# 320 dense tokens and 64 more gathered ones, with all gates built by matmuls, in an encoder step on one core

## The chip, the core and the metric

One core of a Trainium2 chip runs the whole step in one launch. The metric is device time in microseconds (us). The engines are PE (TensorE, with its weight loads PEld), DVE (VectorE), ACT (ScalarE), POOL (GpSimd) and SP (SyncE, which issues transfers). Each works through its own queue in order; semaphores connect them.

## The reference, cut to what matters

544 tokens of width 1024 go through one layer: 512 frames of a new stream (the prompt) and 32 frames of a running one (the sample). The part that the change touches is the second half of the layer:

```python
def peer_block(xb, w_query, keys_1, keys_2, u_tab, v_tab):      # 8 heads, 128 x 128 experts
    qy = (xb @ w_query).reshape(n, 8, 2, 128)
    s1, s2 = scores of the two halves of qy against keys_1, keys_2     # (n, 8, 128) each
    t1, i1 = top_k(s1, 16);  t2, i2 = top_k(s2, 16)
    top, sel = top_k(t1[:, None] + t2[None, :], 16)                    # of 256 pairs
    idx = i1 * 128 + i2 of the chosen pairs                            # 16 experts per head
    g = softmax(top)
    act = gelu(u_tab[idx] . xb)
    return sum over heads and experts of (g * act) * v_tab[idx]

h = layer_norm(alpha * x + token_mixer(x))      # attention and a linear recurrence, merged, projected
y = layer_norm(alpha * h + peer_block(h))
```

A token needs 8 × 16 = 128 of the 16384 experts. All arithmetic is in fp32.

## The kernel before

The tokens are S (32 sample frames) and P0 to P3 (128 prompt frames each). A first mixer runs S, P0 and P1 (288 columns), a second one P2 and P3 (256 columns). A matrix product in full precision is made of three: `split` cuts an operand into a high part (ACT, line 115) and a low part, which is the operand less the high part (line 119, DVE or, for the share `POOL_SHARE`, POOL), and `mm3` (lines 161, 164 and 165) multiplies high by high, low by high and high by low.

For the experts there are two ways. A **dense** token is multiplied with all experts: `up(b)` multiplies block b of table u (128 experts) with the normalized columns of the dense tokens, `hDh` and `hDl`, and takes the gelu; `down(b)` multiplies the result with the gates of this block (zero for experts that were not chosen), splits it, and multiplies with block b of table v. Before, P0, P1 and P2 are dense: 384 columns, 24 matmuls of 384 columns in `up`, 18 of 512 columns in `down`. For a **gathered** token POOL fetches the chosen rows of both tables by an indirect DMA (1 MB for 128 rows), DVE takes a dot product (line 1070), and DVE adds the weighted row to a sum (line 1082). S (packed four times, so 32 steps) and P3 (128 steps) are gathered.

`route(t, h)` finds the 16 experts of head h for the tokens t, mostly on DVE. The gates of the dense tokens have to be brought into the form experts × tokens. Before, there are two ways for that too. For P0 and P1 POOL writes each gate into a zeroed matrix in DRAM, by 256 indirect DMAs (`scatter`, line 998), behind 32 fills with zeros; `down` reads it back as `gt`. For P2 `gate_steps` makes one-hot matrices of four tokens at a time (DVE, tile `hot`, lines 1034 and 1038), multiplies them on TensorE (line 1042) and copies the result out. Routes and builds are put into `bg`, a list from which the matrix work takes a piece now and then at the rates `MIX_RATE` and `OUT_RATE`. The loop `experts` makes `up(it)` and, 29 iterations later (`AHEAD`), `down(it - 29)`:

```python
for it in range(EARLY, NK + AHEAD - LAST):
    if it < NK:
        up(it)
    b = it - AHEAD
    ...
    if b >= 0:
        p = down(b)
        for i in range(NDT):
            p(i)
```

So first only table u is read, then both, then only table v. The subtraction for the low part of both tables (line 1156) is on DVE. A gather is also paced on the load of the iteration's table block.

Of the kernel before, what the change touches and what calls it, by code (L numbers as in the profile page):

```python
# [23 lines left out]
F32 = mybir.dt.float32  # L24
# [9 lines left out]
P = 128  # L34
D = 1024
# [19 lines left out]
POOL_SHARE = (1, 5), (0, 1)  # L55
MIX_RATE = (6, 5), (3, 2)
MERGE_RATE = (1, 3)
OUT_RATE = (3, 2), (1, 1)
# [4 lines left out]
class Tok:  # L63


    def __init__(self, name, col, n, dense=None, prompt=None):
        self.name, self.col, self.n, self.dense, self.prompt = name, col, n, dense, prompt
        self.rep = P // n
        self.nh = H // self.rep
        self.ns = self.nh * TOPK  # L70
        self.done = 0

# [5 lines left out]
         toks=[Tok("S", 0, 32), Tok("P0", 32, 128, 0, 0), Tok("P1", 160, 128, 128, 128)]),  # L78
    dict(c0=288, n=256, p0=256, np=256, off=0,
         att=[Tok("P2", 0, 128, prompt=256), Tok("P3", 128, 128, prompt=384)],  # L80
         toks=[Tok("P2", 0, 128, 256, 256), Tok("P3", 128, 128, None, 384)]),
]
ND = 384
NDT = ND // P
ND0 = TS + ND
NS = 256
GT, GB = 16, 16
FILL, EARLY = 3, 4
AHEAD = 29
# [12 lines left out]
class Build:  # L102
    def __init__(self, tc, A):
        self.tc, self.nc, self.A = tc, tc.nc, A
        self.nsplit = 0
        self.pool_share = (1, 1)
        self.bg, self.tick, self.rate = [], -4, (1, 1)
        self.scatters, self.late, self.ready = {}, [], {}
        self.acts = {}

# [85 lines left out]
    def run(self):  # L196
        with ExitStack() as es:
# [6 lines left out]
            with tc.tile_pool(name="psm", bufs=3, space=PSUM) as self.psm, \  # L204
                    tc.tile_pool(name="kv", bufs=1) as self.kv, \
                    tc.tile_pool(name="wst", bufs=3) as self.wst:
                with tc.tile_pool(name="broA", bufs=1) as bro:
                    self.open(0, lambda s, name: self.keep.tile([P, KD, ND0], F32R, tag="hD" + s, name=name + s)[:, :, :288], bro)
                    self.load_first()
                    self.mixer(0)  # L210
                with tc.tile_pool(name="mTB", bufs=1) as mpool:
                    with tc.tile_pool(name="broB", bufs=1) as bro:
                        self.open(1, lambda s, name: mpool.tile([P, KD, 256], F32R, tag="mT" + s, name=name + s), bro)
# [6 lines left out]
    def open(self, i, tile_, bro):  # L220

        g = GROUPS[i]
        g["mT"] = lambda name: [tile_(s, name) for s in "hl"]
# [6 lines left out]
    def constants(self):  # L230
# [20 lines left out]
        self.iotaK = const.tile([P, 2, NK], F32, name="iotaK")  # L251
        for i, st in enumerate((NK, 1)):
            nc.gpsimd.iota(self.iotaK[:, i], pattern=[[st, NK]], base=0, channel_multiplier=0,
                           allow_small_or_imprecise_dtypes=True)

        self.tcol = const.tile([P, NDT], F32, name="tcol")
        nc.gpsimd.iota(self.tcol, pattern=[[P, NDT]], base=0, channel_multiplier=1,
                       allow_small_or_imprecise_dtypes=True)

        self.sel = const.tile([P, TS], F32, name="sel")  # L260
        nc.vector.tensor_reduce(out=self.sel, in_=self.ident.rearrange("p (g t) -> p t g", t=TS),
                                axis=AX.X, op=OP.add)

        self.G = self.dram.tile([NE * NS, 1], F32, name="gatemat")
        self.G2 = self.dram.tile([P // GT, P, NK * GT], F32, name="gatemat2")
        self.hS = self.dram.tile([ND, D], F32, name="hspill")
        zero = self.vtile(F32, [P, D], "zero")
        nc.gpsimd.memset(zero, 0.0)
        flat = self.G.rearrange("(p n) o -> p (n o)", p=P)
        self.zeroing = []  # L270

        def fill(c):
            self.zeroing.append(self.after_load(nc.sync.dma_start(flat[:, c * D:(c + 1) * D], zero)))
        self.bg += [lambda c=c: fill(c) for c in range(NE * NS // P // D)]
# [70 lines left out]
    def mixer(self, i):  # L345
# [390 lines left out]
    def rows_of_h(self, g, pool):  # L736
        nc, A = self.nc, self.A
        for t in g["toks"]:

            t.h = (self.keep if t.dense is None else pool).tile([P, D], F32, name="h" + t.name)  # L740
# [56 lines left out]
    def scale_rows(self, toks, eng):  # L797

        for t in toks:
            eng.tensor_tensor(out=t.h, in0=t.h, in1=self.g1, op=OP.mult)  # L800
            eng.tensor_tensor(out=t.h, in0=t.h, in1=self.b1, op=OP.add)
            if t.dense is not None:
                self.nc.sync.dma_start(self.hS[t.dense:t.dense + t.n], t.h)
# [541 lines left out]
```

## Time and profile before

| | |
|---|---|
| median of three runs | 1834.27 us (1832.07 to 1834.3) |
| profiled execution | 1832.22 us, span 1830.4 us |
| busy: PE, DVE, ACT, POOL | 1681.0, 1399.3, 866.9, 702.7 us |
| mean granted clock of TensorE | 0.963 |
| bytes moved | 442.97 MB |

The span begins with the first instruction of the profile. The first mixer with its projection and queries lies before about 330 us, the second with its projection from there to about 559, the queries of P2 and P3 to 637, then table u alone to 823, both tables to 1657, and table v with the final normalization to the end.

### The profile page before, as it was taken

Reading aid. Unit: us, or ns where it says so; the run is one execution under the profiler, and the core shown is the slowest. Engines: PE = TensorE matmul, PEld = TensorE weight load, DVE = VectorE, ACT = ScalarE, POOL = GpSimd, SP = SyncE. Lnnn points to the kernel's source line nnn. Section 1 sums busy time; section 2 is a strip of 40 time slices with the busy share of each in tenths; the row PEclk is TensorE's granted clock in tenths of the full one; section 3 lists DMA queues with packets and bytes.
Section 4 is the critical chain, followed back from the end, with each engine's and each line's share of the span. In section 5 each row is a group of like instructions: output and inputs, shape, how many; then the busy total and the mean of one; then the engine's idle time right before and its main releaser. Section 6 shows DMA issues by size and latency. Waiting matters only on the chain.

```text
span 1830.4 us, 26792 instructions
## 1 busy us (share of the span) xinstructions
PE 1681.0 (92%) x9448; PEld 1513.2 (83%) x9448; DVE 1399.3 (76%) x3187; ACT 866.9 (47%) x1723; POOL 702.7 (38%) x463
## 2 busy tenths in 40 slices
PE   8999999994989999919999999999999999998787
PEld 8889879984778999918898799999998989997565
DVE  6634779883976789719999878887888888886667
ACT  7644445782645674504555434443444444332333
POOL 2110236888888888862221112221222222121110
PEclk9999999997998999959999999999999999999999
DMA  9863736674475657649989689889999889897673
GB/s 318 281 233 100 226 99 161 157 164 63 57 185 121 147 117 179 164 105 349 333 297 326 238 321 334 342 339 348 320 333 361 330 313 335 332 345 286 249 263 108
DMA packets 159158, 442.97 MB, mean 242 GB/s; under 512 B 51064, under 2 KB 78376, under 8 KB 137520
## 3 DMA queue, kind: packets, MB, share of 16 engines
q1 hardware_dynamic: 93472, 265.76, 43.3%
q0 software_dynamic: 59904, 167.93, 29.5%
q10 hardware_dynamic: 5648, 7.58, 1.2%
q8 instruction: 74, 1.21, 0.3%
q14 instruction: 60, 0.49, 0.1%
HBM read 409.80 MB, written 31.36 MB: 241 GB/s over the span
## 4 chain that ended last, share of the span: by engine, by line
PE 65%; DVE 7%; DMA 4%; POOL 4%; ACT 4%; issue 2%; SPq 0%; DVEq 0%; ACTq 0%; POOLq 0%
PE y L161 9%; PE y L164 9%; PE u L161 9%; PE y L165 9%; PE u L164 9%; PE u L165 8%; POOL gatemat L998 4%; PE mm L161 3%; PE mm L164 3%; PE mm L165 3%; DMA gat<-peer_uv,idxP 2%; PE y L1042 1%; DVE wl L119 1%; PE x L895 1%; ACT vh L1155 1%
## 5 line engine op out<-in xcount | busy, mean ns | idle before, releaser
L998 POOL DMA_INDIRECT gatemat<-gateP,idxP x256 | 441.9, 1726 | 94.8 <-issue 73.3
L1059 POOL DMA_INDIRECT gat<-peer_uv,idxP x128 | 159.8, 1249 | 601.5 <-DMA ur<-u_chunk 191.4
L165 PE MATMUL u<-hDh,ul 128*128 128x384 f32 x992 | 335.8, 339 | 42.3 <-DVE ul L1156 42.2
L161 PE MATMUL u<-hDh,uh 128*128 128x384 f32 x992 | 339.7, 342 | 9.2 <-DVE hS L1099 4.5
L164 PE MATMUL u<-hDl,uh 128*128 128x384 f32 x992 | 336.3, 339 | 0.0
L161 PE MATMUL y<-vh,pwh 128*128 128x512 f32 x768 | 281.6, 400 | 25.5 <-ACT vh L1155 25.4
L164 PE MATMUL y<-vl,pwh 128*128 128x512 f32 x768 | 301.4, 396 | 0.7 <-DVE vl L1156 0.7
L165 PE MATMUL y<-vh,pwl 128*128 128x512 f32 x768 | 299.6, 396 | 0.0
L119 DVE TENSOR_TENSOR wl<-raw,wh 128x1024 fp32r<-128x1024 f32 (+1 forms) x134 | 164.4, 1229 | 86.9 <-ACT wh L115 86.3
L165 PEld LDWEIGHTS u<-hDh,ul 128*128 128x128 f32 x992 | 187.4, 189 | 43.8 <-DVE ul L1156 43.8
L1070 DVE SCALAR_TENSOR_TENSOR gat<-gat,hP 128x1024 f32<-128x1024 f32 x128 | 156.2, 1221 | 85.1 <-DMA gat<-peer_uv,idxP 85.0
L115 ACT CAST wh<-raw 128x1024 fp32r<-128x1024 f32 (+1 forms) x140 | 145.0, 1039 | 151.7 <-PE mm L164 87.9
L161 PEld LDWEIGHTS u<-hDh,uh 128*128 128x128 f32 x992 | 187.7, 189 | 15.6 <-DVE hS L1099 5.4
L161 PEld LDWEIGHTS y<-vh,pwh 128*128 128x128 f32 x768 | 144.8, 191 | 60.6 <-ACT vh L1155 32.6
L164 PEld LDWEIGHTS u<-hDl,uh 128*128 128x128 f32 x992 | 187.7, 189 | 4.2
L1155 ACT CAST uh<-ur 128x1024 fp32r<-128x1024 f32 x124 | 129.9, 1047 | 104.0 <-DMA ur<-u_chunk 98.4
L1156 DVE TENSOR_TENSOR vl<-vr,vh 128x1024 fp32r<-128x1024 f32 x128 | 155.9, 1220 | 24.0 <-ACT vh L1155 16.3
L165 PEld LDWEIGHTS y<-vh,pwl 128*128 128x128 f32 x768 | 145.3, 189 | 33.9
L1082 DVE SCALAR_TENSOR_TENSOR accP<-gat,actP,accP 128x1024 f32<-128x1024 f32 x127 | 162.4, 1279 | 13.0 <-ACT actP L1073 12.3
L164 PEld LDWEIGHTS y<-vl,pwh 128*128 128x128 f32 x768 | 145.7, 190 | 31.6 <-DVE vl L1156 1.1
L1156 DVE TENSOR_TENSOR ul<-ur,uh 128x1024 fp32r<-128x1024 f32 x124 | 151.1, 1219 | 25.1 <-ACT uh L1155 17.4
L161 PE MATMUL mm<-xTh,wh 128*128 128x288 f32 (+1 forms) x512 | 155.5, 304 | 12.0 <-ACT wh L115 6.8
(366 smaller groups left out, 3310.3 us busy)
## 6 DMA issues: line engine op xcount, KB each, us to landing
vr<-peer_v SPq DMA_DIRECT2D x128, 512.0 KB
ur<-u_chunk SPq DMA_DIRECT2D x124, 512.0 KB
raw<-w_chunk SPq DMA_DIRECT2D x63, 512.0 KB
gatemat<-zero SPq DMA_DIRECT2D x32, 512.0 KB
raw<-w_q SPq DMA_DIRECT2D x32, 512.0 KB
gt<-gatemat SPq DMA_DIRECT2D x128, 128.0 KB
raw<-w_up SPq DMA_DIRECT2D x16, 512.0 KB
raw<-w_out SPq DMA_DIRECT2D x16, 512.0 KB
```

The costliest lines, as they stand in the source:

```text
L115: nc.scalar.copy(h, src)
L119: eng.tensor_tensor(out=l, in0=src, in1=h.bitcast(F32), op=OP.subtract)
L161: first = nc.tensor.matmul(out, lh, rh, start=start, stop=False)
L164: nc.tensor.matmul(out, lh, rl, start=False, stop=False)
L165: return first, nc.tensor.matmul(out, ll, rh, start=False, stop=stop)
L895: nc.tensor.matmul(ps[:, i], qT[:, t.col:t.col + t.n], self.keysT[:, half], start=True, stop=True)
L998: i = nc.gpsimd.indirect_dma_start(out=self.G, out_offset=bass.IndirectOffsetOnAxis(ap=t.idx[:, j:j + 1], axis=0), in_=t.gate[:, j:j + 1], ...
L1059: i = nc.gpsimd.indirect_dma_start(out=r.rearrange("p i d -> p (i d)"), out_offset=None, in_=A["peer_uv"], in_offset=bass.IndirectOffsetOn ...
L1070: nc.vector.scalar_tensor_tensor(out=r[:, 0], in0=r[:, 0], scalar=1.0, in1=t.h, op0=OP.mult, op1=OP.mult, accum_out=a)
L1082: nc.vector.scalar_tensor_tensor(out=v["acc"], in0=r[:, 1], scalar=a, in1=v["acc"], op0=OP.mult, op1=OP.add)
L1155: nc.scalar.copy(h, raw)
L1156: nc.vector.tensor_tensor(out=l, in0=raw, in1=h.bitcast(F32), op=OP.subtract)
```

## The change

- P0 is cut: its first 64 tokens (P0a, packed twice, 64 steps) are gathered, and 320 tokens stay dense. P0's second half goes through `down` with a 128-wide operand that holds low and high side by side, so that two matmuls per half take the place of three, and a block takes 16 matmuls.
- All gates are made by `gate_steps`; scatters, zero fills and `gt` are gone. Of the two one-hot matrices both are made by one DVE operation each (128x512); the product with the gate is made by POOL.
- The steps of S and the first of P0a, the routes of S, P0 and P1 and the builds of P0 and P1 go into the background of the second mixer. The tiles for it lie in `ring`, in the space of `hD`: two slots for gathered rows and one buffer `hot` for the one-hots. The normalized columns of P0 and P1 are kept in DRAM meanwhile (`hN`) and read back before table u.
- In the second mixer POOL takes half of the subtractions of the weights, the memset of `qa` is on DVE, and in `experts` POOL makes the subtraction of table v (all but the last four blocks). `AHEAD` is 36.

```diff
-POOL_SHARE = (1, 5), (0, 1)
-MIX_RATE = (6, 5), (3, 2)
+POOL_SHARE = (1, 5), (1, 2)
+MIX_RATE = (6, 5), (3, 1)
+MIX_GATHER = 1, 3
 MERGE_RATE = (1, 3)
-OUT_RATE = (3, 2), (1, 1)
+OUT_RATE = (3, 2), (2, 1)
...
-ND = 384
+HALF = 64
+ND = 384 - HALF
...
-GT, GB = 16, 16
+GT, GB, UN = 16, 8, 64
-AHEAD = 29
+AHEAD = 36
...
-                (nc.vector if self.first else nc.gpsimd).memset(self.qa[DH:DH + 2], 1.0)
+                nc.vector.memset(self.qa[DH:DH + 2], 1.0)
...
+    def early_rows(self, toks):
+        S, P0, P1 = toks
+        ring = keep.tile([P, 2 * KD * max(ND, 288)], F32R, tag="hD", name="ring")
+        slots = [ring[:, i * 2 * D:(i + 1) * 2 * D].bitcast(F32).rearrange("p (i d) -> p i d", i=2) for i in range(2)]
+        self.row = lambda: slots.append(slots.pop(0)) or slots[-1]
+        work = [p for h in range(S.nh) for p in self.route(S, h)] + [p for h in range(H) for p in self.route(P0, h)]
+        hot = ring[:, 4 * D:5 * D].bitcast(F32)
...
+            work.append(lambda: self.halve(P0, t))
...
+        work += self.gate_steps(P0, vt, self.bank, nc.gpsimd)
+        work += [p for h in range(H) for p in self.route(P1, h)]
+        work += self.gate_steps(P1, vt, self.bank, nc.gpsimd)
+        for t in gathered:
+            self.steps += self.gather_steps(t)
...
-            nc.vector.tensor_tensor(out=B, in0=self.iotaK[:, 1, None].to_broadcast(sh),
-                                    in1=T[:, 1, t0:t0 + 4, None].to_broadcast(sh), op=OP.is_equal)
-            for j in range(4):
-                c = slice(t0 + j, t0 + j + 1)
-                nc.vector.tensor_scalar(out=A[:, j], in0=self.iotaK[:, 0], scalar1=T[:, 0, c], scalar2=T[:, 2, c],
-                                        op0=OP.is_equal, op1=OP.mult)
+            for m, x in ((1, B), (0, A)):
+                nc.vector.tensor_tensor(out=x, in0=self.iotaK[:, None].to_broadcast(sh),
+                                        in1=T[:, m, t0:t0 + 4, None].to_broadcast(sh), op=OP.is_equal)
+            nc.gpsimd.tensor_tensor(out=A, in0=A, in1=T[:, 2, t0:t0 + 4, None].to_broadcast(sh), op=OP.mult)
...
+            eng = nc.gpsimd if name == "v" and not stage else nc.vector
+            eng.tensor_tensor(out=l, in0=raw, in1=h.bitcast(F32), op=OP.subtract)
...
+                    if t.nd == UN:
+                        first = nc.tensor.matmul(o, pw[:, :P], vh[:, cs], start=start, stop=False)
+                        nc.tensor.matmul(o, pw[:, :P], vl[:, cs], start=False, stop=stop)
```

POOL at the beginning of the second mixer, before: the last rows of the scaling of h, then the scatters (line 998), with the memset of qa among them.

```order
L801 TENSOR_TENSOR hS<-hS,b_2399 128x1024
L801 TENSOR_TENSOR hP_2392<-hP_2392,b_2399 128x1024
L801 TENSOR_TENSOR hP_2395<-hP_2395,b_2399 128x1024
L998 DMA gatemat<-gateP_2816,idxP_2815 4194304x1 x16
L998 DMA gatemat<-gateP_2818,idxP_2817 4194304x1 x16
L998 DMA gatemat<-gateP_2816,idxP_2815 4194304x1 x16
L998 DMA gatemat<-gateP_2818,idxP_2817 4194304x1 x16
L998 DMA gatemat<-gateP_2816,idxP_2815 4194304x1 x16
L356 MEMSET qa 2x2048
```

POOL there now: subtractions of weights (wl, line 123) between the gathers of the sample's rows (into ring).

```order
L801 TENSOR_TENSOR hP_2358<-hP_2358,b_2362 128x1024
L123 TENSOR_TENSOR wl<-raw,wh 128x1024 x5
L123 TENSOR_TENSOR rTl<-th,rTh 128x256
L1118 DMA ring<-peer_uv,idxS 128x2048 x2
L123 TENSOR_TENSOR wl<-raw,wh 128x1024 x2
L1118 DMA ring<-peer_uv,idxS 128x2048
L123 TENSOR_TENSOR wl<-raw,wh 128x1024
L1118 DMA ring<-peer_uv,idxS 128x2048
L123 TENSOR_TENSOR wl<-raw,wh 128x1024 x2
```

The scatters and the memset are gone from POOL's queue, and the memset stands on DVE. In all, POOL has 23 subtractions and 48 products with the gate in the second mixer and its projection.

DVE late in the second mixer, now: the last pieces of a route (px, oh, pair), then 34 one-hots (line 1087), which are 17 build steps, then the residual of the sample and the first step of P0a.

```order
L1034 TENSOR_SCALAR pos<-sel 128x16
L1035 SCALAR_TENSOR_TENSOR pos<-pos,sel 128x16
L1046 TENSOR_TENSOR oh<-px,iota_141 128x512
L1047 TENSOR_TENSOR oh<-oh,tif 128x512
L1049 TENSOR_REDUCE pairP_2782<-oh 128x2x16
L1087 TENSOR_TENSOR ring<-iotaK,pairT 128x512 x34
L1172 SCALAR_TENSOR_TENSOR hS,stat2S<-hS,x 32x512 x2
L1132 TENSOR_SCALAR accP0a<-ring,actP0a 128x1024
```

Before, no one-hots stood in this part of DVE's queue; now 96 stand there, for 48 build steps, with 18 heads of routes (13 before), 51 gathered steps (none before) and 28 subtractions of weights (49 before).

POOL in the stage with both tables, before and now: the gathers of P3 had the queue to themselves.

```order
L1059 DMA gat<-peer_uv,idxS 128x2048 x32
L1059 DMA gat<-peer_uv,idxP_6835 128x2048 x128
```

Now the subtractions of table v (line 1233) stand between them.

```order
L1118 DMA gat<-peer_uv,idxP_7319 128x2048
L1233 TENSOR_TENSOR vl<-vr,vh 128x1024
L1118 DMA gat<-peer_uv,idxP_7319 128x2048
L1233 TENSOR_TENSOR vl<-vr,vh 128x1024
L1118 DMA gat<-peer_uv,idxP_7319 128x2048
L1233 TENSOR_TENSOR vl<-vr,vh 128x1024
L1118 DMA gat<-peer_uv,idxP_7319 128x2048
L1233 TENSOR_TENSOR vl<-vr,vh 128x1024 x2
```

The tables' subtractions moved from DVE's queue into POOL's. With `AHEAD` 36 there are 32 iterations with table u alone, which hold 27 of DVE's subtractions, eight heads and the 32 builds of P2; 92 with both tables and about 136 gathered steps; and 32 with table v alone before the last four blocks, with 37 gathered steps left, ten of them behind the last of these iterations.

## Rows read from the trace of the kernel before

**Rows 1.** Windows by stage: start:end, length, busy time and count per engine, PEclk, DMA share, GB/s.

```profile
0.00:330.00 330.00, 312.34 (x2078) 280.12 (x2079) 214.62 (x570) 180.88 (x356) 87.44 (x68) 0.98 0.63 201
330.00:559.00 229.00, 190.07 (x1270) 168.76 (x1268) 170.99 (x630) 132.66 (x275) 194.95 (x114) 0.89 0.59 121
410.00:453.00 43.00, 19.51 (x163) 19.31 (x161) 14.70 (x36) 9.55 (x14) 36.70 (x23) 0.77 0.45 74
...
637.00:823.00 186.00, 142.05 (x881) 139.80 (x882) 126.27 (x434) 84.81 (x148) 147.42 (x88) 0.89 0.60 139
761.00:823.00 62.00, 21.95 (x120) 21.31 (x119) 16.98 (x87) 14.26 (x29) 41.71 (x28) 0.67 0.50 109
823.00:1657.00 834.00, 826.75 (x4121) 747.01 (x4120) 705.45 (x1159) 365.72 (x730) 187.76 (x142) 1.00 0.90 329
1657.00:1830.00 173.00, 135.20 (x545) 103.95 (x543) 123.07 (x226) 53.25 (x103) 18.43 (x16) 0.94 0.62 217
```

**Rows 2.** Window of 50 us inside the stage with both tables (PE, PEld, DVE, ACT, POOL).

```profile
1350.00:1400.00 50.00, 50.00 (x252) 45.36 (x251) 44.20 (x62) 21.70 (x44) 11.67 (x10) 1.00 0.94 342
```

**Rows 3.** The chain of waits near the end: start, length, what.

```profile
1808.85 0.46 PE y L161 x2
```

**Rows 4.** The chain of waits at the first starved stretch.

```profile
449.41 1.55 POOL gatemat L998
...
451.00 1.81 POOL qa L356
```

**Rows 5.** The chain of waits at the second starved stretch.

```profile
810.44 9.84 DMA gg<-gatemat
```

**Rows 6.** Groups by line and shape: busy us, mean ns | idle before, releaser.

```profile
L1034 DVE TENSOR_TENSOR hot<-iotaK,pairT 128x512 f32<-128x512 f32 x32 | 21.9, 684 | 0.3 <-PE y L1042 0.3
...
L1042 PE MATMUL y<-hot 128*128 128x128 f32 x256 | 31.8, 275 | 0.0
...
L1189 DVE TENSOR_TENSOR pwl<-acts,pwh 128x384 fp32r<-128x384 f32 x128 | 70.2, 551 | 22.3 <-ACT pwh L1188 18.1 <-ACT actP L1072 4.1
...
L119 POOL TENSOR_TENSOR wl<-raw,wh 128x1024 fp32r<-128x1024 f32 x6 | 14.4, 2403 | 106.7 <-ACT wh L115 88.7 <-DVE nm L593 18.0
```

**Rows 7.** Timeline of DVE with both tables: start, length, operation.

```profile
1351.93 1.22 DVE L1070 SCALAR_TENSOR_TENSOR gat<-gat,hP 128x1024 f32<-128x1024 f32 x1
1353.07 0.08 DVE L1070 DVE_READ_ACCUMULATOR gat<-gat,hP 128x1 f32 x1
...
1353.75 1.28 DVE L1082 SCALAR_TENSOR_TENSOR accP<-gat,actP,accP 128x1024 f32<-128x1024 f32 x1
1354.95 1.22 DVE L1156 TENSOR_TENSOR vl<-vr,vh 128x1024 fp32r<-128x1024 f32 x1
```

**Rows 8.** Timeline of the end of the first mixer's projection, DVE and POOL.

```profile
253.51 0.46 DVE L795 TENSOR_TENSOR hDl<-hT,hDh 128x288 fp32r<-128x288 f32 x1
...
254.57 9.65 DVE L795 TENSOR_TENSOR hDl<-hT,hDh 128x288 fp32r<-128x288 f32 x4
256.18 5.20 POOL L800 TENSOR_TENSOR hP<-hP,g 128x1024 f32<-128x1024 f32 x2
```

**Rows 9.** Timeline of the first mixer's merge, DVE and POOL.

```profile
184.83 2.41 POOL L119 TENSOR_TENSOR wl<-raw,wh 128x1024 fp32r<-128x1024 f32 x1 [26.89 <-ACT wh L115]
185.07 2.48 DVE L668 SCALAR_TENSOR_TENSOR mTl<-sg,mTh 128x288 fp32r<-128x288 f32 x1 [0.16 <-ACT mTh L667]
```

**Rows 10.** Windows of line 971 alone (once per head of a route).

```profile
330.00:559.00 229.00, 5.36 (x13) 0.89 0.59 121
637.00:684.00 47.00, 2.09 (x5) 1.00 0.59 114
```

**Rows 11.** Window of line 119 alone (subtractions): DVE, POOL.

```profile
330.00:559.00 229.00, 56.24 (x49) 0.00 (x0) 0.89 0.59 121
```

**Rows 12.** Window with five heads of routes, all engines.

```profile
637.00:684.00 47.00, 43.10 (x238) 41.52 (x239) 40.70 (x169) 34.91 (x65) 39.68 (x25) 1.00 0.59 114
```

**Rows 13.** The same window, line 1156 alone on DVE.

```profile
637.00:684.00 47.00, 13.39 (x11) 1.00 0.59 114
```

More of the change, by code (lines that the diff above doesn't have):

```diff
@@ L107, in __init__ @@
         self.bg, self.tick, self.rate = [], -4, (1, 1)
-        self.scatters, self.late, self.ready = {}, [], {}
+        self.late, self.ready = [], {}
         self.acts = {}
+        self.steps, self.pending, self.pace = [], None, None
     def split(self, src, h, l):
@@ new lines, in early_step, with halve @@
+    def early_step(self):
+        if self.row and self.steps:
+            s = self.steps[0]
+            if s.tok.done:
+                self.steps.pop(0)()
+    def halve(self, t, u):
+        nc, n, c = self.nc, u.n, u.ns
+        assert t.done == H
+        other = self.rt.tile([P, c], I32, name="idxo")
+        for dst, i in ((u.idx, 0), (other, 1)):
+            sl = slice(i * c, (i + 1) * c)
+            nc.vector.scalar_tensor_tensor(out=dst[:n], in0=t.pair[:n, 0, sl], scalar=float(NK), in1=t.pair[:n, 1, sl],
+                                           op0=OP.mult, op1=OP.add)
+        nc.gpsimd.tensor_copy(u.gate[:n], t.gate[:n, :c])
+        nc.gpsimd.dma_start(u.idx[n:], other[:n])
+        nc.gpsimd.dma_start(u.gate[n:], t.gate[:n, c:])
+        u.done = H
@@ L828, in out_second, with early_end @@
+    def early_end(self):
+        for i, p in enumerate(self.bg):
+            assert p != self.early_step or not self.steps or self.steps[0].tok is not self.early[0], "sample rows"
+        self.flush()
+        self.row = None
+        for p in self.bg:
+            p()
+        self.bg = []
     def out_second(self):
@@ L901, in route_queries @@
                 nc.scalar.copy(t.sc[m], ps[:, i])
[L902 removed]
+            if half and g is GROUPS[1]:
                 for t in full:
@@ L1173, in down @@
                 out.extend([ybank(i, half) for half in range(2)] for i in range(NDT))
-            gt = pool.tile([P, NS], F32, tag="gt", name="gt", bufs=3)
-            i = nc.sync.dma_start(gt, gates[b * P:(b + 1) * P])
-            load, mm = ups[min(b + AHEAD, NK - 1)]
-            tc.add_manual_dep(i.ins, load.ins.name, ORDER, reason="queue order")
-            for s in [i for c in self.scatters.values() for i in c]:
-                tc.add_manual_dep(i.ins, s.ins.name, SYNC, reason="all heads are in")
@@ L1226, in experts @@
             b = it - AHEAD
-            if b >= -1 and (b + 1) % GB == 0 and b + 1 < NK:
-                assert not build
-                gates_in((b + 1) // GB)
+            if b >= 0 and b % GB == GB // 2 and b + GB < NK:
+                gates_in(b // GB + 1)
             if b >= 0:
                 p = down(b)
-                for i in range(NDT):
+                for i in (1, 2, 0):
                     p(i)
@@ L1265, in experts @@
             stat = pool.tile([P, 7], F32, tag="stat", name="stat", bufs=3)
-            self.residual(P, t.h, out[i], stat)
-            self.finish(P, t.h, stat, A["o_yp"][t.prompt:t.prompt + t.n], pool)
+            halves = out[i]
+            if t.nd < P:
+                halves = []
+                for half in range(2):
+                    y = pool.tile([P, 2, D], F32, tag="gat", name="yraw", bufs=NGAT)[:, 0, :512]
+                    nc.scalar.copy(y, out[i][half])
+                    halves.append(ubank()[:t.nd])
+                    nc.tensor.matmul(halves[half], self.sel[UN], y, start=True, stop=True)
+            self.residual(t.nd, t.h, halves, stat)
+            self.finish(t.nd, t.h, stat, A["o_yp"][t.prompt + t.skip:t.prompt + t.n], pool)
 OUTS = {"o_yp": (TP, D), "o_ys": (TS, D), "o_kp": (TP, DA), "o_vp": (TP, DA), "o_lp": (TP, H), "o_cp": (3, DR),
```

299 lines of the change are left out of this document (168 added, 131 removed).

## The prediction

> **What bounds the kernel now.** I read the windows by stage first, since a share over the whole span mixes stages with different limits [rows 1]. In the long stage with both expert tables (823 to 1657 us) PE is busy for 826.75 of 834 us at full clock, DVE for 705, and POOL for only 188. So PE is the bound there, and 834 us are 45% of the span. A 50-us window shows how an iteration is made: 252 matmuls, which are six iterations of 24 (table u, 384 columns) and 18 (table v, 512 columns), so 8.33 us each [rows 2]. Two table-v matmuls take 0.46 us in the chain of waits [rows 3], 0.23 each, 4.2 for 18; that leaves 4.15 for the 24, 0.173 each. The same window shows DMA at 0.94 busy and 342 GB/s: the transfers are close behind PE.
>
> Two windows show PE starved: 410 to 453 us (busy 19.51 of 43, granted clock 0.77) and 761 to 823 us (21.95 of 62, clock 0.67) [rows 1]. The chain of waits names the cause. In the first, POOL issues scatters of 1.55 us, one behind the other, then at last its memset of qa, for which the attention of mixer B waits [rows 4]. In the second, a 9.84-us load of the gates, which has to follow the last scatter, stands before the first table-v product [rows 5].
>
> The forecast is made against the profiled execution, 1832.22 us (span 1830.4, 1.82 outside it), which lies 0.1% under the median of the runs shown. A change under 0.2% I count as none.
>
> **What a DVE operation costs beside POOL.** The change gives POOL subtractions of 128x1024 that DVE did. POOL takes 2.40 us for one [rows 6]; DVE's step from a gather's sum to the next operation in the queue is 1.20, and for its dot product 1.14 (1353.75 to 1354.95 and 1351.93 to 1353.07) [rows 7]. I take 1.14 to 1.15 for a DVE subtraction of that size as well. Moved work would be free if the engines were independent. They aren't: a DVE subtraction hDl of 288 columns takes 0.46 us just before POOL starts its run of h times g, and four of them, with what lies between, take until 264.2 once it runs: 9.65 us for x4, each beginning or ending as a POOL operation ends [rows 8]. DVE's mTl, of the same 288 columns, takes 2.48 us under a single POOL subtraction and ends 0.3 us behind it [rows 9]. In all seven overlaps that I found of a DVE operation with two SBUF operands and a POOL tensor operation, DVE stood still to POOL's end. So from the rows I add POOL's time to DVE's, in part. [...]
>
> **Second mixer and projection (330 to 559 us).** Before: 229 us, DVE 171 [rows 1]. DVE gets the following.
> - Routes. 13 heads ran here [rows 10], now 18. From 637 to 684 us DVE is busy 40.70 us with five heads [rows 10, 12] and 11 table subtractions of 13.39 in sum [rows 13]: (40.70−13.39)/5 = 5.5 per head, +27.5.
> - Gathered steps, 51 of them (32 sample, 19 of P0a): 1.14+1.20 = 2.34 each [rows 7], +119.
> - One-hots, 96 of 128x512, at 0.684 less the 0.07 by which queued operations overlap [rows 6, 7], 0.61: +59.
> - Subtractions. 49 ran on DVE [rows 11], now 28: 21×1.15 = −24.
>
> That makes 352 us of DVE, more than the whole stage lasted. DVE becomes the bound, and PE (190 busy) waits. Then three additions. (1) Seventeen build steps stand back to back in DVE's and PE's order, all in one one-hot buffer (the order of DVE in the section on the change). Each is 2×0.68 on DVE, POOL's product with the gate (128x512; by 2.40 for double the width at least 1.2, at most 2.40; I take 1.3, near the proportional value), four matmuls of at least 0.12 (31.8 us for 32 steps of eight before [rows 6], so 0.5 to 1.0 a step), and handovers: 3.9 us against 1.2 in the sum, so 17×2.7 = +46. With a free chain it would be 0. (2) POOL's 21 subtractions are 50 us; half of them charged to DVE gives +25 (0 to 50). (3) The other 31 steps wait in the same way unless mixer work stands between them: 0 taken, at most 31×2.7 = 84. So 423, taken as 425, from 352 to 532. The qa wait is gone in this. Against 229: **+196** (+123 to +303).
>
> **Around it.** Before the second mixer (0 to 330 us) 16.8 MB of zero fills disappear; PE idles there for 18 us [rows 1]: **−5** (0 to −18). From 559 to 637, P0's and P1's normalized columns come back from DRAM only when the ring is free, 1.6 MB, some 5 us at 342 GB/s, and DVE's queue drains first: **+8** (0 to 25).
>
> **Table u alone (637 to 823 us).** Before 186, of which 62 was the scatter wait. Now 32 iterations. A 320-column matmul I scale to 0.144 (by 320/384), so 24 are 3.47, 111 in all, and 32 build steps of up to 1.0 make the PE floor 143. DVE: 27 subtractions (31), 8 heads (44), 64 one-hots (39), 114 in sum; plus POOL's 32 products at 1.3 (42), locked against them: 156. I take 165, **−21** (143 to 186).
>
> **Both tables.** 92 iterations instead of 99. PE: 24×0.144 + 16×0.232 = 7.18. DVE: one subtraction 1.14, gates and the low half of the weights at 320 columns, 0.42 each (from 0.551 less 0.07 at 384 [rows 6]), and 136 gathered steps over 92 iterations, 1.48×2.34 = 3.46: 5.44. POOL's subtraction adds 2.40, if all is locked: 7.84. If only the operations with two SBUF operands of 128x1024 are locked, 7.0. Transfers: two tables 1.05 MB, gathers 1.48×1.05, gates 0.16, about 2.8 MB, at 342 GB/s 8.2 us. [...] Three queues of about equal length wait on each other a little: 8.1, 745 us. **−89** (7.18 gives −173, 9.0 gives −6).
>
> **Closing (1657 us to the end).** Before 173 with 29 iterations; now 32 and the last four tables. PE needs 16×0.232 = 3.7 per iteration. But 37 gathered steps are left; 27 of them stand among the 32 iterations: 27/32×2.34 + 2.40 + two operations of 0.4 that can lie partly beside POOL: 5.1, 163 us. Then ten gathered steps (23), the last four tables' products (15) and the finish (26): 227, **+54** (168, if POOL costs nothing, to 253).
>
> Sum: −5+196+8−21−89+54 = **+143**, so **1975 us**.
>
> **Rivals.**
> (a) *POOL's work is free for DVE.* Then the second mixer is 375 (+146), the u stage 146 (−40), both tables go at PE's pace with a little loss, 7.4 (−153), and the closing 168 (−5): with +8 and −5 a sum of −49, **1783**, faster. For it: POOL idles for 646 of 834 us in the longest stage, and PE is its bound. Against it: [rows 8, 9]. Its 192 us against the forecast are 50 in the second mixer, 19 in the u stage, 64 in both tables and 59 in the closing; if POOL costs DVE less than a quarter of what I charge (49 of 192), the time falls below that of before.
> (b) *No lock, but the transfers hold the iteration at 7.9 to 8.25 us.* Then both tables gain 75 to 107 instead of 153: **1829 to 1861**. For it: 0.94 busy and 342 GB/s [rows 2].
> (c) *POOL, DVE and the gathers wait for each other in order.* A gather waits in POOL's queue for a free buffer, which DVE frees, and the next subtraction of table v stands behind it, for which PE waits. Then 9.0 per iteration (−6), the second mixer 500 (+271), closing 253 (+80), the rest +24: about **2200**. For it: POOL's queue now alternates the two (the order of POOL in the section on the change).
>
> **Chances.** Forecast 0.55 (own range 1890 to 2060), (a) 0.17, (b) 0.13, (c) 0.15. (b) gives a little to faster and to no change. Faster 0.20, no change 0.03, slower 0.77. The range, 1800 to 2110, leaves out half of (a) and two thirds of (c).
>
> **What would show it.** Right: from 330 us a stage of some 420 us with DVE busy over 80% of it and PE under 60%; DVE operations of 128x1024 over 2 us where POOL subtracts; iterations above 7.8 us with PE waiting for vl from POOL. Wrong: iterations at 7.2 to 7.4 with PE still 98% busy (a), or gathers and table loads named as what PE's inputs wait for (b). The forecast falls above all if the DVE load of 352 us in the second mixer is spread so that PE loses less than I say, or if POOL's product with the gate is far from 1.3.

## The result

The changed kernel takes 2695.69 us (median of 4 runs, 2692.04 to 2699.08) against 1834.28 before: a ratio of 1.469, 95% interval 1.465 to 1.473. Slower was forecast, but by 143 us; it is 861. The time is far above the upper end of the range, 2110.

By stage, from the first and last products with the tables in each trace (us):

| | start to first table-u product | table u alone | both tables | from there to the end | span |
|---|---|---|---|---|---|
| before | 638 | 185 | 834 | 173 | 1830.4 |
| forecast of the difference | +199 | −21 | −89 | +54 | +143 |
| after | 995 | 263 | 1166 | 271 | 2694.8 |
| difference measured | +357 | +78 | +332 | +98 | +864.4 |

Every stage is longer than forecast, and the largest miss is where a gain was forecast. The windows of the changed kernel (start:end, length, then busy us and count of PE, PEld, DVE, ACT and POOL, granted clock, DMA share, GB/s) answer to [rows 1]:

```profile
460.00:533.00 73.00, 2.51 (x17) 1.91 (x15) 64.50 (x211) 31.84 (x74) 23.97 (x18) 0.53 0.58 196
...
715.00:800.00 85.00, 36.08 (x135) 29.49 (x135) 27.94 (x55) 12.57 (x37) 21.27 (x25) 0.52 0.18 63
...
995.00:1100.00 105.00, 93.36 (x665) 90.28 (x666) 100.61 (x163) 53.56 (x119) 49.33 (x32) 0.97 0.46 156
1100.00:1258.00 158.00, 92.00 (x389) 83.32 (x388) 79.50 (x296) 60.50 (x111) 5.78 (x3) 0.76 1.10 302
1258.00:2424.00 1166.00, 827.22 (x3645) 710.65 (x3644) 624.70 (x706) 332.57 (x726) 401.63 (x229) 0.83 1.06 347
2424.00:2694.00 270.00, 161.62 (x598) 114.16 (x597) 191.23 (x253) 76.44 (x189) 116.71 (x64) 0.88 0.64 227
```

With both tables no engine is the bound: PE is busy 71%, DVE 54%, POOL 34%. The DMA engines are (1.06 of their time, as the times of the packets in the record add up). What they move is on the page, in the part on transfers and the part on issues (queue and kind: packets, MB, share; then issue, count, KB each, median us to landing):

```profile
q1 hardware_dynamic: 467392, 430.38, 52.9%
...
gg<-gatemat SPq DMA_DIRECT2D x156, 1280.0 KB, 11.9
vr<-peer_v SPq DMA_DIRECT2D x128, 512.0 KB, 8.8
ur<-u_chunk SPq DMA_DIRECT2D x124, 512.0 KB, 11.9
```

The kernel needs 16 blocks of gates, and loads 156. In `experts` the call that loads block 0 stands behind the builds, under a condition that stays true once the builds are done:

```python
if not self.bg:
    ...
    del build[:k]
    if not build:
        gates_in(0)
```

So from then on block 0 is loaded again in every iteration. In SP's queue these loads stand partly earlier than in the loop: here two between two loads of table u, late in the stage mostly one:

```profile
1496.27 6.90 SPq L1230 DMA_DIRECT2D ur<-u_chunk  x1
1503.28 0.37 SPq L1230 DMA_DIRECT2D vr<-peer_v  x1
1503.70 6.67 SPq L1286 DMA_DIRECT2D gg<-gatemat  x2
1510.47 9.38 SPq L1230 DMA_DIRECT2D ur<-u_chunk  x1
```

The list of waits in the whole execution (engine and line, what it waited for, total us, times, longest) shows who pays: the cast of table u comes late to PE.

```profile
PEld u L165 <- ACT uh L1231: 387.7, 94, 8.6
POOL gat L1118 <- DMA ur<-u_chunk: 354.7, 44, 35.5
PE u L165 <- ACT uh L1231: 350.8, 89, 8.2
```

The second mixer is another matter. The waits between 390 and 910 us:

```profile
PE x L1092 <- POOL ring L1089: 152.9, 46, 6.5
...
POOL ring L1089 <- DVE ring L1087: 109.9, 27, 18.9
...
DVE ring L1087 <- PE x L1092: 74.5, 27, 3.7
PE x L1074 <- DVE pairP L1049: 72.9, 2, 64.2
```

Line 1074 is the transposes of the chosen pairs, at the head of the builds of P0. They stand in PE's queue ahead of the attention, and DVE has not made P0's routes: PE stands for 64.2 us in one piece (460 to 533 us above, 2.51 of 73 busy). The other three rows are a ring of waits, the build chain. The timeline of one link of it, line 1087 the one-hots, 1089 the product with the gate, 1092 the matmuls:

```profile
741.18 1.29 DVE L1087 TENSOR_TENSOR ring<-iotaK,pairT 128x512 f32<-128x512 f32 x2 [3.35 <-PE x L1092]
741.84 1.12 POOL L1100 DMA_DIRECT2D gatemat<-stage  x2 [2.84 <-ACT stage L1097]
742.98 1.06 POOL L1089 TENSOR_TENSOR ring<-ring,pairT 128x512 f32<-128x512 f32 x1
...
744.09 2.07 PE L1092 MATMUL x<-ring 128*128 128x128 f32 x8 [2.95 <-POOL ring L1089]
...
746.20 1.29 DVE L1087 TENSOR_TENSOR ring<-iotaK,pairT 128x512 f32<-128x512 f32 x2 [3.73 <-PE x L1092]
```

One step after the other, 5.0 us apart, of which each engine works 1 to 2 and waits 3. The eight matmul passes take 2.07, 0.26 each, where they took 0.12 before [rows 6]. The granted clock in this stretch is 0.52, and PE was busy only 36 of 85 us; before, in the builds from 690 to 757 us, it was 1.00 with PE busy 67 of 67.

### The profile page after: what moved, and what is told of

Its sections match the earlier page's. It is cut to its first block, busy times and chain, and to the rows that moved or that the text cites. A ratio compares the mean times of both kernels' runs of the same rounds, so it can differ in the third digit from the quotient of the medians.

```text
span 2694.8 us, 27706 instructions
## 1 busy us (share of the span) xinstructions
PE 1884.1 (70%) x9590; PEld 1628.3 (60%) x9590; DVE 1658.9 (62%) x3111; ACT 974.2 (36%) x2105; POOL 829.0 (31%) x524
## 2 busy tenths in 40 slices
DMA packets 511068, 688.81 MB, mean 256 GB/s; under 512 B 15736, under 2 KB 421960, under 8 KB 482256
## 3 DMA queue, kind: packets, MB, share of 16 engines
q1 hardware_dynamic: 467392, 430.38, 52.9%
## 5 line engine op out<-in xcount | busy, mean ns | idle before, releaser
L165 PE MATMUL u<-hD,uh 128*128 128x320 f32 x992 | 387.7, 391 | 353.2 <-ACT uh L1231 350.8
L165 PEld LDWEIGHTS u<-hD,uh 128*128 128x128 f32 x992 | 247.7, 250 | 391.3 <-ACT uh L1231 387.7
L1233 POOL TENSOR_TENSOR vl<-vr,vh 128x1024 fp32r<-128x1024 f32 x124 | 323.7, 2610 | 417.1 <-ACT vh L1231 242.1
L169 PE MATMUL u<-hD,ul 128*128 128x320 f32 x992 | 385.7, 389 | 58.3 <-DVE ul L1233 58.1
L168 PE MATMUL u<-hD,uh 128*128 128x320 f32 x992 | 371.8, 375 | 0.0
L169 PEld LDWEIGHTS u<-hD,ul 128*128 128x128 f32 x992 | 243.9, 246 | 91.9 <-DVE ul L1233 91.9
L168 PEld LDWEIGHTS u<-hD,uh 128*128 128x128 f32 x992 | 247.3, 249 | 0.4
L168 PE MATMUL y<-vl,pw 128*128 128x512 f32 x512 | 206.4, 403 | 20.2 <-POOL vl L1233 20.1
L165 PE MATMUL y<-vh,pw 128*128 128x512 f32 x512 | 190.5, 405 | 38.6 <-ACT vh L1231 38.6
L169 PE MATMUL y<-vh,pw 128*128 128x512 f32 x512 | 202.4, 395 | 0.0
L1092 PE MATMUL x<-ring 128*128 128x128 f32 x384 | 95.2, 426 | 152.9 <-POOL ring L1089 152.9
L1260 DVE TENSOR_TENSOR pw<-acts,pw 128x320 fp32r<-128x320 f32 x128 | 97.9, 765 | 145.4 <-ACT pw L1259 145.4
L1092 PEld LDWEIGHTS x<-ring 128*128 128x128 f32 x384 | 81.8, 314 | 168.6 <-POOL ring L1089 168.5
```

What stands on the lines that cost most here:

```text
L165: first = nc.tensor.matmul(out, lh, rh, start=start, stop=False)
L168: nc.tensor.matmul(out, lh, rl, start=False, stop=False)
L169: return first, nc.tensor.matmul(out, ll, rh, start=False, stop=stop)
L1092: nc.tensor.matmul(ps[:, j * NK:(j + 1) * NK], B[:, j], A[:, j], start=True, stop=True)
L1233: eng.tensor_tensor(out=l, in0=raw, in1=h.bitcast(F32), op=OP.subtract)
L1260: nc.vector.tensor_tensor(out=pl, in0=a, in1=ph.bitcast(F32), op=OP.subtract)
```

## Experiments

The first theory after the result: the repeated loads set the expert stages, and PE's order and the build chain the second mixer (R). The rival: POOL's subtractions and the waits between the queues, which the prediction had as its term and as rival (c), only larger (L).

**One load of block 0.**

```diff
-                if not build:
+                if not build and 0 not in gg:
                     gates_in(0)
```

> Only the first call of the load of gate block 0 in the expert loop is kept; the changed kernel issues it again in every iteration after the builds are done (156 loads of 1280 KB in its trace, 16 needed). Theory R (these loads set the expert stages): the stage with both tables falls from 12.7 us per iteration to 7.9 to 8.4, the rest of the table-u stage and the closing lose what they waited for gates, and the time falls by 400 to 500 us to 2200 to 2300. Rival L (POOL's subtractions and the order of the queues set the iteration): it stays above 10.5 us and the time above 2500. Either way the second mixer keeps its 580 us, so it stays above 2150.

Measured: 2269.24 us (ratio to before 1.237, 1.232 to 1.243), 426 us less. Both tables: 812 us, 8.83 per iteration, more than the 7.9 to 8.4 expected; table u alone 194. The windows of these two stages, table u alone first:

```profile
992.00:1186.00 194.00, 163.00 (x1052) 156.09 (x1053) 179.98 (x478) 109.44 (x227) 58.67 (x37) 0.92 0.58 186
1186.00:1998.00 812.00, 697.94 (x3646) 610.83 (x3646) 668.95 (x686) 324.60 (x725) 421.96 (x226) 0.97 0.84 309
```

The bytes fall from 688.81 to 505.29 MB, that is 183.5, or 140 loads of 1.31 MB. R holds for the greater part of what these stages lost. The closing doesn't change (269), nor does the second mixer.

**The same number of loads, small.**

```diff
                 if not build and 0 not in gg:
                     gates_in(0)
+                elif not build:
+                    less = ggate("gg").rearrange("p (q b t) -> p q b t", b=GB, t=GT)
+                    nc.sync.dma_start(less[:, 0].rearrange("p b t -> p (b t)"), self.G[0, :, :GB * GT])
```

> The repeated loads stay in number, queue and buffer, but move 64 KB each instead of 1280 KB. If the bytes were the cost (1.3 MB more per iteration in packets of 512 B): within 40 us of the run with one load. If SP's queue standing at each load for a free gate buffer was the cost: at least 100 us over that run.

Measured: 2287.93 us in one run, 19 over the run with one load. So it is what the loads move, not their place in SP's queue. Bytes and packets fall together here (a repeated load has 2576 packets in the changed kernel and 144 in this run, from the packets of queue q1: 467392, 126912 and, with one load, 106752), so this run doesn't say which of the two counts.

**Table v's subtraction on DVE.**

```diff
-            eng = nc.gpsimd if name == "v" and not stage else nc.vector
+            eng = nc.vector
```

> As the run with one load of gate block 0, and table v's subtraction on DVE instead of POOL. If DVE stands still while POOL subtracts (the lock as predicted: 2.4 to 2.6 us of POOL for 1.14 of DVE), the iteration with both tables falls by 0.4 to 1 us and the closing by 30 to 60 us against that run: 60 to 140 us less. If POOL's work is free for DVE, DVE has 1.14 us more per iteration and the time is the same or up to 60 us longer. If the transfers bound the iteration, only the closing changes.

Measured (with one load of block 0): 2157.88 us (1.178, 1.172 to 1.183), 111 less. Both tables take 732 us, 7.96 per iteration instead of 8.83, and the closing 242 instead of 269 (27 less, where 30 to 60 were expected). DVE has one subtraction more per iteration and the kernel is faster. The timeline with POOL's subtraction (one load) shows how:

```profile
1498.84 2.41 POOL L1233 TENSOR_TENSOR vl<-vr,vh 128x1024 fp32r<-128x1024 f32 x1 [1.64 <-issue]
1498.93 3.40 DVE L1134 SCALAR_TENSOR_TENSOR accP<-gat,actP,accP 128x1024 f32<-128x1024 f32 x1 [1.40 <-ACT actP L1127]
```

DVE's sum, begun 0.09 us after POOL's subtraction, takes 3.40 instead of 1.28 us, and ends 1.08 behind its end: it ran after it. Over the stage with both tables the mean of this operation is, first with POOL's subtraction, then in this run with DVE's:

```profile
L1134 DVE SCALAR_TENSOR_TENSOR accP<-gat,actP,accP 128x1024 f32<-128x1024 f32 x90 | 208.5, 2316 | 56.0 <-ACT actP L1127 56.0
```

```profile
L1134 DVE SCALAR_TENSOR_TENSOR accP<-gat,actP,accP 128x1024 f32<-128x1024 f32 x90 | 115.1, 1279 | 4.4 <-ACT actP L1127 4.4
```

PE feels it at DVE's other work, the low part of table u. Its waits for that in the same stage, again with POOL's subtraction and then with DVE's:

```profile
PE u L169 <- DVE ul L1233: 95.0, 54, 2.9
```

```profile
PE u L169 <- DVE ul L1233: 9.2, 13, 1.5
```

**The same edit backwards, on the kernel before.**

```diff
-            nc.vector.tensor_tensor(out=l, in0=raw, in1=h.bitcast(F32), op=OP.subtract)
+            eng = nc.gpsimd if name == "v" and not stage else nc.vector
+            eng.tensor_tensor(out=l, in0=raw, in1=h.bitcast(F32), op=OP.subtract)
```

> The kernel before, with table v's subtraction on POOL (all but the last four blocks) and nothing else. If POOL's reads shut out DVE's operations with two SBUF operands: DVE and POOL together then need 5.5 + 2.4 = 7.9 us of an iteration of 8.33, gathers and products wait for each other, and the time grows by 20 to 110 us. If POOL is free for DVE: PE still sets the stage, within 10 us, or less in the closing.

Measured: 2036.18 us (1.109, 1.106 to 1.113), 203 more, nearly twice the upper end. By stage, both tables 891 instead of 834, and the closing 196 instead of 173: 80 us, within the range expected, and put down to the lock (DVE standing still while POOL subtracts, and POOL while DVE works): with both tables DVE is busy 789 us instead of 705, though it has 99 subtractions less, its low part of table u takes 1.38 us in the mean instead of 1.22, and POOL's subtraction 2.97 instead of 2.40. The rest is another wait: table u begins at 806 instead of 638, and of these 168 us the stage with table u alone gives back 42 (143 instead of 185). Timeline rows of POOL's queue, then of SP's:

```profile
795.51 1.55 POOL L998 DMA_INDIRECT gatemat<-gateP,idxP  x1 [0.30 <-issue]
797.13 2.34 POOL L1157 TENSOR_TENSOR vl<-vr,vh 128x1024 fp32r<-128x1024 f32 x1
```

```profile
799.50 0.33 SPq L1154 DMA_DIRECT2D vr<-peer_v  x1
799.92 13.21 SPq L1154 DMA_DIRECT2D ur<-u_chunk  x4
```

The first subtraction stands in POOL's queue behind all scatters. SP waits with a load of table v until it is done, and behind that load stand the loads of table u, for which PE waited 167 us.

**The builds of P0 and P1 out of the second mixer.**

```diff
-        work += self.gate_steps(P0, vt, self.bank, nc.gpsimd)
         work += [p for h in range(H) for p in self.route(P1, h)]
-        work += self.gate_steps(P1, vt, self.bank, nc.gpsimd)
...
-        build = self.gate_steps(dense[-1], built, gbank, nc.sync)
+        build = [s for t in dense for s in self.gate_steps(t, built, gbank, nc.sync)]
...
-BUILD = 5, 2
+BUILD = 4, 1
```

> As the run with one load of gate block 0, and the 48 build steps of P0 and P1 moved out of the second mixer into the loop over table u, four steps per iteration. If the build chain in PE's queue (one buffer, DVE to POOL to PE and back) starves the second mixer: the stage from 330 us to the first expert product falls from 580 to 400 or less, the table-u stage grows by 60 to 110, net 70 to 140 us less. If DVE's load alone sets that stage: it falls only by the 59 us of one-hots, which come back later, net within 30 us.

Measured (with one load): 2122.24 us (1.159, 1.154 to 1.164), 147 less. The first product with table u comes at 750 instead of 992 us, 242 earlier; table u alone then takes 234 instead of 194, both tables 827 instead of 812 and the end 308 instead of 269. The net gain is a little over the upper end of 140, and the builds cost 40 us with table u, less than the 60 expected.

The 242 aren't the builds alone. The list of background work has a gathered step behind every third piece, so fewer pieces take fewer steps along. Line of the dot product up to table u (two records a step), with one load and then in this run:

```profile
330.00:992.00 662.00, 67.67 (x102) 0.70 0.48 163
```

```profile
330.00:750.00 420.00, 53.98 (x82) 0.80 0.61 202
```

So 41 steps run there instead of 51, and the closing has 48 left instead of 37. The builds and ten gathered steps together cost 242 us before table u.

**Two one-hot buffers.**

```diff
-        vt = lambda name: hot if name == "hot" else self.vtile(F32, [P, D], name)
+        hots = [hot, keep.tile([P, D], F32, name="hot2")]
+
+        def vt(name):
+            if name != "hot":
+                return self.vtile(F32, [P, D], name)
+            hots.append(hots.pop(0))
+            return hots[-1]
...
-NV = 8
+NV = 7
```

> As the run with one load of gate block 0 (2269 us), with two one-hot buffers for the early builds in turn instead of one (and 7 instead of 8 of the general work buffers, to make room). If a build step is long because the next one waits for the one buffer (DVE to POOL to PE and back, 5.0 us a step in the run of 17), steps overlap and fall towards PE's own 2.1 us: the second mixer is 80 to 140 us shorter. If the steps wait for DVE's other work or for late routes instead, it changes by less than 40 us.

Measured: 2220.88 us in one run, 48 less than with one load; the first product with table u comes at 937 instead of 992, 55 earlier. That is between the two expectations (80 to 140, or less than 40): the buffer is a part of the chain's cost. The general work buffers, 7 instead of 8, changed with it.

**The product with the gate on DVE.**

```diff
-            nc.gpsimd.tensor_tensor(out=A, in0=A, in1=T[:, 2, t0:t0 + 4, None].to_broadcast(sh), op=OP.mult)
+            nc.vector.tensor_tensor(out=A, in0=A, in1=T[:, 2, t0:t0 + 4, None].to_broadcast(sh), op=OP.mult)
```

> As the run with one load of gate block 0, with the product with the gate on DVE instead of POOL in all 80 build steps. If POOL's product and its handover sit in the chain (1.0 us and a handover, against 0.6 on DVE): 15 to 50 us less in the second mixer. If DVE's load sets the stage: 48 times 0.6 = 29 us more there, and 20 more in the table-u stage.

Measured: 2224.39 us in one run, 45 less, 33 of it before table u. POOL out of the chain is worth more than its product costs on DVE. Whether by the handover or by the lock between the two, this run doesn't tell.

**Three edits at once, and all subtractions of the second mixer on DVE** (`POOL_SHARE = (1, 5), (0, 1)`).

> One load of gate block 0, table v's subtraction on DVE, the builds of P0 and P1 moved into the table-u loop, and all subtractions of the second mixer on DVE. If the first two gains add up (111 and 147 us against 2269): 2011 without the last edit. With the lock as found, 21 POOL subtractions of 2.4 us less for 21 DVE ones of 1.2 give another 0 to 25 us: 1985 to 2015. If they were free for DVE, it is 2020 to 2040. In no case is it below 1834.

Measured: 1997.9 us (1.088, 1.085 to 1.092). The sum of the gains gives 2011, so they add up to within 13 us, which may be the fourth edit's; it wasn't run alone. The window of the second mixer to the first product with table u, in this run:

```profile
327.00:735.00 408.00, 311.60 (x1869) 271.54 (x1868) 364.91 (x1201) 268.66 (x543) 59.67 (x47) 0.80 0.62 207
```

DVE is now busy 365 of 408 us and PE 312. So DVE comes close to being the bound that the prediction named, once the builds don't stand in PE's queue.

**384 dense tokens again, on top of these.**

```diff
-HALF = 64
+HALF = 0
...
-AHEAD = 36
+AHEAD = 26
-BUILD = 4, 1
+BUILD = 6, 1
```

> The run with all three edits and the second mixer's subtractions on DVE, with 384 dense tokens again: no P0a gathered, 24 matmuls of 384 columns and 18 of 512 per iteration, builds six per iteration, and AHEAD 26 for space. If the 64 gathered steps cost DVE more (64 times 2.34 = 150 us) than PE gains by 320 columns (1.15 us in each of 92 iterations = 106): 30 to 80 us less than 1998. If PE sets the time where both tables run: up to 60 us more.

Measured: 1938.1 us (1.057, 1.054 to 1.060), 60 less. Both tables take 845 us for 102 iterations, 8.28 each, and the end 122 instead of 280. So the 64 gathered tokens lose more on DVE than PE gains, and on top of the other edits this part of the change is a loss of some 60 us. The lead of table u, 26 instead of 36 blocks, and the rate of the builds changed with it.

**The memset alone, in the kernel before.**

```diff
-                (nc.vector if self.first else nc.gpsimd).memset(self.qa[DH:DH + 2], 1.0)
+                nc.vector.memset(self.qa[DH:DH + 2], 1.0)
```

> The kernel before, with the memset of qa on DVE in the second mixer and nothing else. If the wait at 410 to 453 us is lost time: 30 to 42 us less than before. If POOL's chain of 256 scatters (1.85 us each, 474 us from 331 on) sets the first product with table v anyhow: the wait only moves to the second starved stretch, and the time changes by less than 8 us.

Measured: 1832.72 us, ratio 0.999 (0.997 to 1.001). No change, and the windows say where the wait went. They are the two starved stretches of [rows 1]:

```profile
410.00:453.00 43.00, 42.35 (x324) 38.05 (x323) 41.37 (x156) 31.10 (x80) 36.60 (x22) 1.00 0.63 135
...
761.00:823.00 62.00, 8.08 (x29) 7.82 (x30) 8.09 (x30) 2.13 (x5) 39.69 (x27) 0.52 0.41 81
```

The first is full now. The second, 21.95 us busy before, has 8.08: PE comes 32 us earlier to table u (606 instead of 638) and waits there for the same last scatter: the first product with table v is at 822 instead of 823.

**Half of the scatters, in the kernel before.** P1's gates are built as P2's, `NS` is 128, the memset is on DVE.

```diff
-NS = 256
-GT, GB = 16, 16
+NS = 128
+GT, GB = 16, 8
-BUILD = 5, 2
+BUILD = 5, 1
...
-            if t.dense == NS:
+            if t.dense is not None and t.dense >= NS:
...
-        build = [s for t in dense if t.dense == NS for s in self.gate_steps(t, pool, gbank)]
+        build = [s for t in dense if t.dense >= NS for s in self.gate_steps(t, pool, gbank)]
```

> The kernel before, with P1's gates built by one-hot matmuls in the table-u loop as P2's are (five build steps per iteration), only P0's scattered (128 instead of 256), and the memset of qa on DVE. If POOL's chain of scatters sets the first product with table v, its end moves from 806 us to some 570 and both starved stretches go: about 75 us less for them (the 42 and 38 of the 62 us), plus 32 build steps of 1.8 us of DVE and 1.0 us of PE where DVE and PE are both busy: 30 to 60 us. Net 15 to 60 us less than before. If the table-u stage needs its 186 us for DVE's routes anyway: within 10 us of before.

Measured: 1820.32 us, ratio 0.9943 (0.9917 to 0.9969). So it is about 0.6% faster than the kernel before, 12 us, a little under the 15 to 60 expected. POOL's last scatter is at 580 us. The window of table u alone:

```profile
622.00:817.00 195.00, 187.35 (x1231) 184.87 (x1231) 184.59 (x591) 110.78 (x196) 6.65 (x7) 0.98 0.59 205
```

The starved stretches are gone, and the 32 further builds fill most of what that freed: the stage takes 195 us instead of 185, and begins 16 earlier.

**The one-hots with one DVE and four ACT operations, on top of that.**

```diff
-            for j in range(4):
-                c = slice(t0 + j, t0 + j + 1)
-                nc.vector.tensor_scalar(out=A[:, j], in0=self.iotaK[:, 0], scalar1=T[:, 0, c], scalar2=T[:, 2, c],
-                                        op0=OP.is_equal, op1=OP.mult)
+            nc.vector.tensor_tensor(out=A, in0=self.iotaK[:, 0, None].to_broadcast(sh),
+                                    in1=T[:, 0, t0:t0 + 4, None].to_broadcast(sh), op=OP.is_equal)
+            for j in range(4):
+                nc.scalar.mul(A[:, j], A[:, j], T[:, 2, t0 + j:t0 + j + 1])
```

> As the kernel before with P1's gates built by matmuls too, and in every build step the second one-hot made by one DVE operation of 128x512 and multiplied with the gate by four ACT operations, in place of four DVE operations of 128x128. In the table-u stage DVE is busy 185 of 195 us there, 70 of them in those four operations; one of 0.6 us in their place saves 0.5 a step, 64 steps, 30 us or so, and ACT (111 of 195 busy) takes some 55 us more. If DVE sets that stage: 15 to 30 us less than that run, 1790 to 1805. If the chain DVE to ACT to PE sets the step: the same or up to 40 us more.

Measured: 1843.07 us, ratio 1.0055 (1.0033 to 1.0076): 23 us over the run above, as the second of the two expectations has it, and 15 to 30 less was the first. From 622 to 760 us this run has PE busy 137.84 of 138 us and DVE 109.10, so neither DVE nor the chain set this stretch and the saving on DVE was worth nothing; and before the first product with table v PE waits 23.1 us for ACT's cast of the gated activations (pwh). Why ACT is late there wasn't tested.

## Why the prediction was wrong, step by step

**Both tables (−89 forecast, +332 measured). This step failed.** It counted 0.16 MB of gates per iteration and 2.8 MB in all. The loop issues the load of block 0, 1.31 MB, again in each iteration, which stood in the diff, and that queue's transfers were never counted. 426 us of the 720 by which the forecast missed are this, shown by removing it: 354 in this stage and 69 with table u alone. What is left is 8.83 us per iteration, between the 8.1 taken and the 9.0 of the upper end. It is longer than any of the term's three queues: PE is busy 7.59 us of it, DVE 7.27 with its standstills (7.84 if all is locked), and the DMA share is 0.84. So the lock was not priced too low, but the waiting of the queues on each other was: 8.1 adds nothing for it, since it is less than the 8.2 that the term has for the transfers. PE waits 95 us for DVE's low part of table u, and not for vl from POOL, as the prediction's sign had it. Taking POOL's subtraction away gives 0.87 per iteration (8.83 to 7.96), and with DVE's the iteration is between PE's 7.18 and the 8.2 of the transfers:

```profile
1177.00:1909.00 732.00, 687.78 (x3644) 616.22 (x3643) 613.29 (x780) 323.00 (x725) 199.09 (x136) 0.96 0.94 344
```

**Second mixer and what follows it to table u (+199 forecast, +357 measured).** DVE's load was sized a little low, and it didn't set the stage. The windows that compare are the queries of P2 and P3 before, and everything from 330 us to table u in the changed kernel:

```profile
559.00:637.00 78.00, 74.58 (x560) 73.53 (x560) 58.90 (x175) 49.61 (x114) 66.72 (x38) 0.96 0.65 149
```

```profile
330.00:995.00 665.00, 400.80 (x2267) 352.78 (x2265) 483.58 (x1345) 280.35 (x652) 202.65 (x152) 0.69 0.48 163
```

The term's 352 us, the 25 for the lock and the 59 of the queries make 436; 484 were measured, 73% of the 665 us. The step that failed is what was added for the builds: 46 us for 17 of the 48 steps and 0 for the other 31, beside 59 of one-hots in DVE's load. With ten gathered steps (23 us) that is 128 us for what the run with later builds takes out of this stretch, and it took out 242.

Three things make up the builds' price. All 48 steps form the chain, not 17: the row of PE's waits for POOL's product counts 46. A step takes 4.6 to 5.0 us in the stretch shown and 5.5 to 8.4 between 533 and 580 us, not 3.9; PE's part alone is 2.07 us at the granted clock of 0.52, against 1.0 at most. And PE's queue stands 64 us for the first pair of P0 before any step. The prediction speaks of PE's order for the 17 steps; that the attention stands behind P0's builds was not priced. How much of the 242 each of the three took was not separated; a second buffer brings table u 55 us forward, POOL's product on DVE 33.

**The removal of the qa wait, priced inside the mixer's term.** It is worth nothing by itself: the memset alone changes the time by −0.1% (−0.3 to 0.1). Both starved stretches are one cause, POOL's 474 us of scatters, seen at two places. What helped in these runs was fewer scatters, and the builds that replace them take most of it back.

**Table u alone (−21, +78).** With one load of block 0 it takes 194 us, +9: the upper end was 186. DVE is busy 180 of them, where the term had 156 with POOL's products in it, and PE 163 over a floor of 143.

**Closing (+54, +98).** Unchanged by the repeated loads (269 us). 37 gathered steps were left, as counted. DVE is busy 191 of the 270 us and POOL 117, and DVE's sum (line 1134) takes 2.07 us there in the mean instead of 1.28; with table v's subtraction on DVE the closing is 242. The term was 44 us short, and its upper end, +80, was 18 short.

**The lock between POOL and DVE**, as the prediction takes it from its rows, was the right mechanism: the 3.40 us of the row above against 1.28 agree with it, and so do 2.32 against 1.28 in the mean of that operation. The overlaps that the prediction counts are of operations with two operands. Of those with one, not all stay free: under POOL's subtraction of 416.13 us (last section) a MAX8 of DVE takes 0.28 us, as it does elsewhere, but a TENSOR_SCALAR of 128x16 with one input, whose median is 0.17, takes 2.09 and ends 0.02 behind POOL's end.

**The rivals.** (a) is refuted: with POOL's work costing DVE nothing, moving it back to DVE could not have gained 111 us. (b) had the right resource, the transfers, but from bytes that nobody needed. (c) is nearest in time to the run with one load (2200 against 2269), by waits in order (9.0 per iteration, 8.83 measured), though its largest one is in PE's queue and not in POOL's.

The parts add up as follows: 2696, less 426 (repeated loads), 111 (table v's subtraction), 147 (later builds, and the ten steps that move with them), 13 (what all four edits have beyond the sum) and 60 (64 gathered tokens), is 1938, and 105 us above before remain. What is still different there is the second mixer with the sample's gathered rows and the routes, and 96 build steps in place of 32, not separated.

## What to carry to other kernels

Count the transfers that each queue issues against those that are needed, per iteration, before pricing any engine: here one line of a loop moved 183 MB that nothing needed. Background work that PE takes part in should be ready when PE's queue reaches it: here three transposes, 0.90 us in all (line 1074, from 525.82), were reached before their input was ready, and PE stood for 64.2 us with the attention behind them. And when a stall has a long chain on another engine behind it, ask whether removing the place where it shows moves the end or only the wait: here the memset's move filled 410 to 453 us and left the first product with table v at 822 instead of 823.

## What the runs showed of the hardware that wasn't expected

POOL waits for DVE as DVE does for POOL, as far as these rows show it. In the second mixer of the changed kernel a subtraction of 128x1024, 2.40 us before [rows 6], takes 2.96 and 4.23 us on POOL where DVE's operations with two inputs lie in the same stretch (beside the first, a subtraction of line 123 from 405.98 to 407.20):

```profile
406.46 2.96 POOL L123 TENSOR_TENSOR wl<-raw,wh 128x1024 fp32r<-128x1024 f32 x1
416.13 4.23 POOL L123 TENSOR_TENSOR wl<-raw,wh 128x1024 fp32r<-128x1024 f32 x1 [6.71 <-ACT wh L119]
```

DVE beside the second of them:

```profile
415.74 1.27 DVE L1134 SCALAR_TENSOR_TENSOR accS<-ring,actS,accS 128x1024 f32<-128x1024 f32 x1
...
416.94 1.21 DVE L1124 SCALAR_TENSOR_TENSOR ring<-ring,hS 128x1024 f32<-128x1024 f32 x1
...
418.08 0.28 DVE L990 MAX8 tv<-mscr 128x8 f32<-128x128 f32 x1
418.29 2.09 DVE L1034 TENSOR_SCALAR pos<-sel 128x16 uint32<-128x16 uint32 x1
```

POOL's subtraction ends at 420.36, 2.4 us after 417.96, so it seems to have run only when DVE's sum and product were about done (418.15).

And in the stretch where PE waits for the build chain it is also slower when it does work: from 715 to 800 us, with PE busy 36 of 85, the granted clock is 0.52 and a matmul pass takes 0.26 us; before, from 690 to 757 us, with PE busy throughout, the clock is 1.00 and the same pass takes 0.12. So the eight passes of a step take 2.07 us instead of 0.99, and the starved build chain is stretched a second time.
